# Seven products of quarters for eight in the second products of two feed-forwards, interleaved with the next chunk's first product

## The chip, the cores and the metric

The kernel runs on one core of a Trainium2 chip. The metric is device time in microseconds (us), the median of several executions. Lower is better.

## The reference, cut to what matters

The program is two transformer blocks over 256 tokens with a model width of 2048. Only the two feed-forwards matter here. Everything is float32.

```python
# first block: D_FF = 8192
z = rmsnorm(h, norm2_w) @ mlp_w1                   # 2048 x 8192
h = h + jnp.square(jax.nn.relu(z)) @ mlp_w2        # 8192 x 2048
...
# second block: D_FF_2 = 5632
g, u = jnp.split(x @ w_in, 2, axis=-1)             # 2048 x 11264
y = (jax.nn.silu(g) * u) @ w_out                   # 5632 x 2048
x = layer_norm(ALPHA * x + y, ln_g[l, 2], ln_b[l, 2])
```

## The kernel before

**Float32 in three products.** Every weight and every activation is split into two float32r parts, hi and lo, with hi + lo equal to the value. A product is hi·hi + hi·lo + lo·hi, three matmuls that accumulate in one PSUM bank.

**Weights.** `Stream` (lines 31 to 75) holds the weight tiles in the order in which the products use them, 128 x 1024 elements (two blocks of 128 rows by 512 columns, 512 KB) for nearly all. SyncE loads them into 3 buffers (`RAW`), ScalarE casts a tile to `whi` (line 63), VectorE subtracts to get `wlo` (line 64). There are 4 buffers of each part (`SPLIT`), and splitting runs at most 3 tiles ahead of the products (`LOOK`). So a tile's cast waits until TensorE has finished the tile four places earlier.

**First products** are `TJob`s (lines 221 to 258): weights stationary, out[feature, token]. For a block of 128 rows and 128 features there are two matmuls, one with 512 moving columns (whi times both parts of the tokens, line 257) and one with 256 (wlo times the high part, line 256). A bank is left by `join` (line 351): ScalarE copies one half of it to `ev`, VectorE adds the other half. `relu2` (line 925) then takes relu squared on VectorE and splits the result into `hid`; `gate_f` and `up_f` (lines 1442, 1449) do silu and the product of the second block and split into `fh`. These chains are posts: `side.pump` issues one step of each at a time between the matmuls.

**Second products** are `NJob`s (lines 261 to 317): activations stationary, weights moving, out[token, feature]. One tile takes 12 matmuls of 512 columns (2 row blocks, 2 token tiles of 128, 3 matmuls each, lines 273 to 275). `add_scaled` (line 942), `add_part` (line 938), `first_rows` (line 1466) or `final_rows` (line 1497) add a finished bank to the residual `res` on VectorE.

**Order.** The order of the program is written out by hand in the list `prog`; each engine does its own instructions in that order. The hidden width goes in chunks of 1024 features (8 in the first block, 5 and one of 512 in the second), and chunk c+1's first product stands before chunk c's second product:

```python
    up(0)
    for c in range(NCH):
        if c + 1 < NCH:
            up(c + 1)
        if c == NCH - 1:
            Name(new_xt, "x3t")
        down(c, c == NCH - 1)
```

`last_rows` (line 1470) prepares the last LayerNorm: it clears a tile `gb`, loads ln_g and ln_b rows into it and ln_g for all partitions into `row`, and splits `gb` into `ro`. It is issued before the last but one second product.

## Time and profile before

| | |
|---|---|
| three runs | 2546.81, 2547.54, 2548.10 us (median 2547.54) |
| profiled execution, its span from the first to the last instruction | 2543.4 us |
| what lies around the span, if that execution took the median | 4.1 us |
| TensorE matmul busy | 2520.1 us, 99% of the span |
| VectorE busy | 1611.4 us, 63% |
| ScalarE busy | 1190.8 us, 47% |
| mean granted TensorE clock | 0.997 of full speed |
| bytes moved | 472.93 MB, 186 GB/s |

TensorE's busy time counts overlapping matmuls once and is near 100% wherever matmuls follow each other. How fast they follow is read from their start times. VectorE's mean durations of one instruction are also longer than the step from one to the next where nothing is waited for, since neighbours overlap a little.

### The profile page before, as it was taken

The numbers are of one execution on the slowest core, as the hardware profiler recorded it, in microseconds if no ns is written. First come the engines' busy times: TensorE is split into PE (matmuls) and PEld (weight loads), VectorE is DVE, ScalarE is ACT, GpSimd is POOL, SyncE is SP. The second block draws the span as 40 slices with busy tenths as digits, with TensorE's granted clock in tenths as the row PEclk, the third lists the DMA queues.
The fourth block names the chain that finished last, engine by engine and source line by source line (L and its number), as shares of the span: only waits on it lengthen the run. The fifth ranks groups of instructions, "written<-read, shape, count | busy, mean of one in ns | idle before, by whom it ended". The sixth has DMA issues, their size and how long they took to land.

```text
span 2543.4 us, 34921 instructions
## 1 busy us (share of the span) xinstructions
PE 2520.1 (99%) x13581; PEld 2160.9 (85%) x13581; DVE 1611.4 (63%) x2240; ACT 1190.8 (47%) x1680; POOL 60.6 (2%) x82
## 2 busy tenths in 40 slices
PE   8999999999999999999999999999999999999998
PEld 8897888888888888888888888888788888888886
DVE  5655666556656656768656667767775555565557
ACT  5444444444444444444544565555544444444443
POOL 0000000000000000000000000020200000000000
PEclk9999999999999999999999999999999999999999
DMA  8444555555566565555555555665566666566664
GB/s 278 133 160 147 164 190 189 191 191 191 183 198 197 190 193 190 187 168 181 172 174 166 166 185 188 224 218 165 190 190 190 193 189 195 186 197 189 193 193 156
DMA packets 132326, 472.93 MB, mean 186 GB/s; under 512 B 14992, under 2 KB 16352, under 8 KB 131888
## 3 DMA queue, kind: packets, MB, share of 16 engines
q1 hardware_dynamic: 128624, 460.77, 56.5%
q0 software_dynamic: 3104, 9.32, 1.3%
q8 instruction: 106, 1.74, 0.3%
q10 hardware_dynamic: 432, 0.61, 0.1%
q14 instruction: 60, 0.49, 0.1%
HBM read 468.54 MB, written 2.10 MB: 185 GB/s over the span
## 4 chain that ended last, share of the span: by engine, by line
PE 96%; DVE 2%; DMA 1%; ACT 1%; issue 0%; POOL 0%; SPq 0%; DVEq 0%; ACTq 0%; POOLq 0%
PE acc L257 34%; PE acc L256 17%; PE acc L273 11%; PE acc L274 11%; PE acc L275 11%; PE acc L253 2%; PE acc L247 2%; PE acc L249 2%; PE acc L248 2%; DMA wraw<-in_weights_dram 1%; PE acc L254 1%; DVE wlo L64 1%; PE aux L1160 0%; PE aux L1090 0%; ACT whi L63 0%
## 5 line engine op out<-in xcount | busy, mean ns | idle before, releaser
L64 DVE TENSOR_TENSOR wlo<-wraw,whi 128x1024 fp32r<-128x1024 f32 (+1 forms) x870 | 1055.6, 1219 | 856.0 <-ACT whi L63 854.6
L63 ACT CAST whi<-wraw 128x1024 fp32r<-128x1024 f32 (+1 forms) x870 | 905.8, 1047 | 1060.4 <-PE acc L257 507.7
L257 PE MATMUL acc<-x5t,whi 128*128 128x512 f32 x1320 | 462.8, 394 | 1.0 <-DVE x5t L490 1.0
L256 PE MATMUL acc<-x5t,wlo 128*128 128x256 f32 x1320 | 366.7, 278 | 0.0
L257 PE MATMUL acc<-x3t,whi 128*128 128x512 f32 x960 | 339.4, 395 | 0.0
L257 PE MATMUL acc<-x2t,whi 128*128 128x512 f32 x960 | 335.9, 394 | 0.0
L257 PEld LDWEIGHTS acc<-x5t,whi 128*128 128x128 f32 x1320 | 247.8, 188 | 54.7 <-DVE x5t L490 1.4
L256 PE MATMUL acc<-x3t,wlo 128*128 128x256 f32 x960 | 272.0, 283 | 0.0
L256 PE MATMUL acc<-x2t,wlo 128*128 128x256 f32 x960 | 266.1, 277 | 0.0
L256 PEld LDWEIGHTS acc<-x5t,wlo 128*128 128x128 f32 x1320 | 248.1, 188 | 4.3 <-DVE wlo L64 0.2
L257 PEld LDWEIGHTS acc<-x2t,whi 128*128 128x128 f32 x960 | 180.0, 187 | 39.0
L257 PEld LDWEIGHTS acc<-x3t,whi 128*128 128x128 f32 x960 | 180.1, 188 | 38.6
L273 PE MATMUL acc<-whi,hid 128*128 128x512 f32 x512 | 199.5, 390 | 0.0
L274 PE MATMUL acc<-wlo,hid 128*128 128x512 f32 x512 | 199.2, 389 | 0.0
L275 PE MATMUL acc<-whi,hid 128*128 128x512 f32 x512 | 199.2, 389 | 0.0
L256 PEld LDWEIGHTS acc<-x3t,wlo 128*128 128x128 f32 x960 | 181.0, 189 | 3.2
L256 PEld LDWEIGHTS acc<-x2t,wlo 128*128 128x128 f32 x960 | 180.2, 188 | 2.9
L274 PE MATMUL acc<-wlo,fh 128*128 128x512 f32 x352 | 137.1, 389 | 0.5 <-DVE wlo L64 0.5
L273 PE MATMUL acc<-whi,fh 128*128 128x512 f32 x352 | 137.0, 389 | 0.0
L275 PE MATMUL acc<-whi,fh 128*128 128x512 f32 x352 | 136.9, 389 | 0.0
L275 PEld LDWEIGHTS acc<-whi,hid 128*128 128x128 f32 x512 | 96.1, 188 | 20.0
L274 PEld LDWEIGHTS acc<-wlo,hid 128*128 128x128 f32 x512 | 96.1, 188 | 19.9
(481 smaller groups left out, 3577.5 us busy)
## 6 DMA issues: line engine op xcount, KB each, us to landing
wraw<-in_weights_dram SPq DMA_DIRECT2D x859, 512.0 KB, 3.6
row<-in_ln_g_dram POOLq DMA_DIRECT2D x12, 256.0 KB, 6.5
wraw<-in_weights_dram SPq DMA_DIRECT2D x8, 336.0 KB, 2.9
ht<-in_hT_dram SPq DMA_DIRECT2D x8, 272.0 KB, 5.1
res<-in_x_dram SPq DMA_DIRECT2D x2, 1024.0 KB, 8.6
row<-in_ln_b_dram POOLq DMA_DIRECT2D x8, 256.0 KB, 9.3
out_dram<-res SPq DMA_DIRECT2D x6, 256.0 KB, 2.7
pw<-in_pool_w_dram SPq DMA_DIRECT2D x1, 1024.0 KB, 8.7
```

What stands on the lines that cost most here:

```text
L63: nc.scalar.copy(hi, t)
L64: nc.vector.tensor_tensor(lo, t, hi.bitcast(F32), op=OP.subtract)
L247: mm(b[:m, :n], wh, x[:, 0], start=first, stop=False)
L248: mm(b[:m, :n], wh, x[:, 1], start=False, stop=False)
L249: mm(b[:m, :n], wl, x[:, 0], start=False, stop=last)
L253: mm(bv, wh, x, start=True, stop=False, skip_group_check=True)
L254: mm(bv[:, 1], wl, x[:, 0], start=False, stop=False, skip_group_check=True)
L256: mm(bv[:, 1], wl, x[:, 0], start=False, stop=False, skip_group_check=True)
L257: mm(bv, wh, x, start=False, stop=last, skip_group_check=True)
L273: mm(b, xh, hi[:, j, :n], start=first, stop=False)
L274: mm(b, xh, lo[:, j, :n], start=False, stop=False)
L275: mm(b, xl, hi[:, j, :n], start=False, stop=last)
```

## The change

It replaces the plain second product by one with 7 products of quarters in place of 8. Take 8 row blocks of the hidden features (two halves, A11 A12 over the first 128 tokens, A21 A22 over the others) and 1024 output columns (weight quarters B11 B12 B21 B22, each 4 row blocks by 512 columns). Sums of quarters of A and of B are multiplied, and the seven results are added into the four output quarters, some through a common term `u` that is added at the end. This is done for one of the two column pairs in 7 of the 8 chunks of the first feed-forward and for both pairs in 5 of the 6 chunks of the second, 17 pairs in all.

- A quarter product is two weight tiles ("quarter units") of 6 matmuls each. The four B quarters are loaded into held buffers (`Ring`, five slots, tags g, f0, f1, e3). VectorE adds or subtracts quarters in place (`Stream.sums`, line 85, 128x1024 each, 8 per pair), and each of the 14 units is split into whi and wlo as every tile is (8 tiles per pair before).
- The sums of the hidden features, `four_sums` (lines 516 to 519), are formed on VectorE as features finish, and split by `convert` (lines 1124, 1127) into `spa`, `spb`, `spc` and `l0a`/`l0b`.
- The next chunk's first product is cut into "up units" of one feature block (one tile of 8 row blocks by 128 columns, 16 matmuls). `merge` mixes them with the quarter units; in the first block the last 4 of 16 go with 8 "row units" of the other two column groups, 12 matmuls each.
- Each finished quarter leaves its bank through `put`: 7 VectorE reads per pair where there were 4.
- ALPHA moves into `affine`, which is finished earlier, and `last_rows` now stands right before the last second product.

```diff
+    def pre(self, i):
+        it = self.items[i] if i < len(self.items) else None
+        if isinstance(it, Item) and not it.summed and all(q.t is not None for q in it.quads):
+            self.sums(it.pre)
+            it.summed = True
...
+                    nc.scalar.copy(hi, t)
+                    self.pre(self.s + 1)
+                    nc.vector.tensor_tensor(lo, t, hi.bitcast(F32), op=OP.subtract)
+                    if held:
+                        self.sums(it.post)
...
+        def unit(name, h, bank, first, then):
+            def run():
+                hi, lo = stream.next()
...
+                for j in range(2):
+                    xh, xl = lhs(name, 2 * h + j)
+                    mm(b, xh, hi[:, j], start=first and h == 0 and j == 0, stop=False, skip_group_check=True)
+                    mm(b, xh, lo[:, j], start=False, stop=False, skip_group_check=True)
+                    mm(b, xl, hi[:, j], start=False, stop=h == 1 and j == 1, skip_group_check=True)
+                    if h == 1 and j == 1:
+                        put(then, b)
+                    side.pump()
+            return run
...
+                ("s1", "y", True, "-22", lambda h: Item(b12[h], pre=[(b12[h], b11[h], add)])),
+                ("a11", "x", True, "u", lambda h: Item(b11[h])),
+                ("s2", "u", True, "u+", lambda h: Item(b12[h], pre=[(b12[h], b22[h], add)])),
+                ("s4", "y", False, "-12", lambda h: Item(b22[h])),
+                ("a12", "x", False, "+11", lambda h: Item(b21[h], post=[(b21[h], b12[h], add)])),
+                ("s3", "y", True, "-22", lambda h: Item(b12[h], pre=[(b12[h], b11[h], sub)])),
+                ("a22", "y", False, "+21", lambda h: Item(b21[h]))):
...
+    def merge(head, first, second, tail):
+        n = len(second) - tail
+        done = 0
+        for k, u in enumerate(second):
+            upto = len(first) if k >= n else min(len(first), head + (len(first) - head) * k // max(n - 1, 1))
+            prog.extend(first[done:upto])
+            done = upto
+            prog.append(u)
...
+    def middle(c):
+        Name(set_hid, c + 1, FCH)
+        ups = up_parts(c + 1)
+        down = seven("mlp_w2", FCH * c, 0, mring, lambda name, j: quarter(sums, hid[c], name, j), put_scaled(c))
+        merge(2, ups[:SHARE], down, 0)
+        rows = [u for g in (2, 3) for u in row_units("mlp_w2", FCH * c, g, lambda kb: hid[c][:, kb], add_scaled)]
+        merge(1, ups[SHARE:], rows, 2)
...
+    SEVEN = range(NCH - 1)
+    SHARE = 12
...
+    up()
+    for c in SEVEN:
+        middle(c)
+    Call(add_common_scaled)
+    Name(new_xt, "x3t")
+    down(NCH - 1)
...
+        down = [x for p in range(2) for x in
+                seven("w_ffn_out_2", 8 * c, 1024 * p, ring, lambda name, j: quarter(fh, fh[c], name, j), put_rows(c, p))]
+        merge(2, up_units(c + 1), down, 2)
...
-    ffn_up(0)
-    for c in range(len(chunks)):
-        if c + 1 < len(chunks):
-            ffn_up(c + 1)
-        if c == len(chunks) - 2:
-            Name(last_rows)
-        ffn_down(c)
+    ffn_up()
+    last = len(chunks) - 1
+    Name(lambda: side.finish(tk["affine"]))
+    for c in range(last):
+        ffn_middle(c)
+    Call(add_common)
+    Name(last_rows)
+    n_job("w_ffn_out_2", range(8 * last, 8 * last + 4), grp, lambda kb: fh[last][:, kb - 8 * last], final_rows, tail=2)
```

**Place 1, start of the first feed-forward: VectorE's queue at the end of chunk 0's first product.** `ev` is a feature block just finished, `hid` its split. Before:

```order
L64 TENSOR_TENSOR wlo<-wraw,whi 128x1024 x7
L360 TENSOR_TENSOR ev<-acc,ev 128x256
L928 SCALAR_TENSOR_TENSOR ev<-ev 128x256
L360 TENSOR_TENSOR ev<-acc,ev 128x256
L928 SCALAR_TENSOR_TENSOR ev<-ev 128x256
L373 TENSOR_TENSOR hid<-ev,hid 128x256
```

Now (`l0c` and `l1c` are the earlier feature block put together again from its parts, `sf` the sums of features):

```order
L551 TENSOR_TENSOR hid<-ev,hid 128x256
L1167 TENSOR_TENSOR l1c<-hid 128x256
L516 TENSOR_TENSOR sf<-ev,l1c 128x128
L517 SCALAR_TENSOR_TENSOR sf<-sf,l1c 128x128
L518 SCALAR_TENSOR_TENSOR sf<-ev,sf 128x128
L519 TENSOR_TENSOR sf<-l1c 128x128
L129 TENSOR_TENSOR wlo<-wraw,whi 128x1024
L1127 TENSOR_TENSOR spa<-sf,spa 128x4x128
```

These are the last of four such groups. `spa`, which the first quarter unit s1 reads, stands behind all four; only two up units stand between the end of the first product and s1.

**Place 2, a later chunk of the first feed-forward, around units a12 and s3 of the mixed stretch: VectorE's queue.** Before, at the end of a first product with the whole next group of tiles behind it:

```order
L360 TENSOR_TENSOR ev<-acc,ev 128x256
L928 SCALAR_TENSOR_TENSOR ev<-ev 128x256
L373 TENSOR_TENSOR hid<-ev,hid 128x256 x2
L64 TENSOR_TENSOR wlo<-wraw,whi 128x1024 x7
L360 TENSOR_TENSOR ev<-acc,ev 128x256
```

Now (`quads` and `quad...` are the held B quarters, L85 their sums, L1215 a put):

```order
L129 TENSOR_TENSOR wlo<-quads,whi 128x1024
L85 TENSOR_TENSOR quads<-quads,quade_4127 128x1024
L551 TENSOR_TENSOR hid<-ev,hid 128x256
L129 TENSOR_TENSOR wlo<-quads,whi 128x1024
L85 TENSOR_TENSOR quads<-quads,quade_4127 128x1024
L1215 SCALAR_TENSOR_TENSOR res<-aux_4406,nr,res 128x512
L85 TENSOR_TENSOR quade_4127<-quade_4127,quadf_3476 128x1024
L129 TENSOR_TENSOR wlo<-wraw,whi 128x1024
```

Sums, a put and posts now stand between the wlo of one tile and that of the next.

**Place 3, the end of the second feed-forward: VectorE's queue.** Before, the preparation of the last LayerNorm stood among the posts of the last first product, a whole second product earlier:

```order
L360 TENSOR_TENSOR ev<-acc,ev 128x256
L1452 TENSOR_TENSOR ev<-ev,sg 128x256
L1477 MEMSET gb 64x2048
L1483 MEMSET l0a 128x64
L1484 MEMSET l0a 128x1
```

Now the last s3 and a22 (`aux_22431` is their bank; a22's matmuls add into it behind the put of L1841):

```order
L129 TENSOR_TENSOR wlo<-wraw,whi 128x1024
L538 TENSOR_TENSOR ev<-acc,ev 128x256
L1803 TENSOR_TENSOR ev<-ev,l1c 128x256
L1841 SCALAR_TENSOR_TENSOR res<-aux_22431,res 128x512
L129 TENSOR_TENSOR wlo<-wraw,whi 128x1024
L551 TENSOR_TENSOR fh<-ev,fh 128x256
L129 TENSOR_TENSOR wlo<-wraw,whi 128x1024
L1839 TENSOR_TENSOR res<-aux_22431,res 128x512
L1849 TENSOR_TENSOR res<-res,l1a 128x512 x3
L1849 TENSOR_TENSOR res<-res,l1b 128x512 x3
L1865 MEMSET gb 64x2048
```

and behind the small memsets:

```order
L129 TENSOR_TENSOR wlo<-wraw,whi 128x1024 x2
L1888 TENSOR_TENSOR res<-acc,res 128x512
L1891 BN_STATS st<-res 128x6
L1893 TENSOR_TENSOR res<-res,row 128x512
L1888 TENSOR_TENSOR res<-acc,res 128x512
```

The product with `row` (L1893) waits for a load that GpSimd issues behind the five loads into `gb`, which wait for the memset. In all 13407 matmuls become 13203.

## Rows read from the trace of the kernel before

**Rows 1.** Page, part 1: span; busy time, share and instructions of each engine.

```profile
span 2543.4 us, 34921 instructions
...
PE 2520.1 (99%) x13581; PEld 2160.9 (85%) x13581; DVE 1611.4 (63%) x2240; ACT 1190.8 (47%) x1680; POOL 60.6 (2%) x82
```

**Rows 2.** Page, part 4: chain of waits that ended last, share by engine.

```profile
PE 96%; DVE 2%; DMA 1%; ACT 1%; issue 0%; POOL 0%; SPq 0%; DVEq 0%; ACTq 0%; POOLq 0%
```

**Rows 3.** Busy time by stretch, the two feed-forwards: length, PE, PEld, DVE, ACT, POOL, clock.

```profile
352.00:1042.00 690.00, 690.00 (x3520) 587.34 (x3519) 425.61 (x522) 306.42 (x391) 0.00 (x0) 1.00 0.59 190
1830.00:2490.00 660.00, 660.00 (x3536) 567.66 (x3535) 387.73 (x470) 303.19 (x408) 4.60 (x9) 1.00 0.61 192
```

**Rows 4.** Timeline of TensorE, second product: start, us; 21 matmuls from first to last.

```profile
1000.24 0.39 PE L273 MATMUL acc<-whi,hid 128*128 128x512 f32 x1
...
1005.00 0.39 PE L273 MATMUL acc<-whi,hid 128*128 128x512 f32 x1
```

**Rows 5.** Timeline of TensorE, first product: 16 pairs apart, then the next job's start.

```profile
374.91 0.40 PE L257 MATMUL acc<-x2t,whi 128*128 128x512 f32 x1
...
380.45 0.40 PE L257 MATMUL acc<-x2t,whi 128*128 128x512 f32 x1
...
382.07 0.39 PE L253 MATMUL acc<-x2t,whi 128*128 128x512 f32 x1
```

**Rows 6.** VectorE by line and shape: count, busy us, mean ns, idle before.

```profile
L64 DVE TENSOR_TENSOR wlo<-wraw,whi 128x1024 fp32r<-128x1024 f32 x859 | 1047.0, 1224 | 849.6 <-ACT whi L63 848.2
...
L944 DVE SCALAR_TENSOR_TENSOR res<-acc,rq,res 128x512 f32<-128x512 f32 x56 | 39.3, 743 | 0.0
...
L1379 DVE TENSOR_TENSOR res<-res,row 128x512 f32<-128x512 f32 x16 | 10.9, 684 | 0.0
...
L1104 DVE TENSOR_TENSOR pb<-pb,l1b 128x128 f32<-128x128 f32 x1 | 0.3, 292 | 0.0
```

**Rows 7.** Timeline of VectorE, instructions behind each other without a wait.

```profile
2471.96 3.50 DVE L64 TENSOR_TENSOR wlo<-wraw,whi 128x1024 fp32r<-128x1024 f32 x3 [0.52 <-ACT whi L63]
2475.38 1.28 DVE L940 TENSOR_TENSOR res<-acc,res 128x512 f32<-128x512 f32 x2
```

**Rows 8.** Timeline of VectorE, end of the first feed-forward's first t_job.

```profile
381.73 0.42 DVE L360 TENSOR_TENSOR ev<-acc,ev 128x256 f32<-128x256 f32 x1
...
382.52 0.42 DVE L360 TENSOR_TENSOR ev<-acc,ev 128x256 f32<-128x256 f32 x1
...
383.32 0.42 DVE L373 TENSOR_TENSOR hid<-ev,hid 128x256 fp32r<-128x256 f32 x1
383.65 0.42 DVE L360 TENSOR_TENSOR ev<-acc,ev 128x256 f32<-128x256 f32 x1
...
385.10 1.23 DVE L64 TENSOR_TENSOR wlo<-wraw,whi 128x1024 fp32r<-128x1024 f32 x1 [0.57 <-ACT whi L63]
```

**Rows 9.** Timeline of ScalarE, the same place.

```profile
383.43 0.41 ACT L371 CAST hid<-ev 128x256 fp32r<-128x256 f32 x1
...
384.01 1.05 ACT L63 CAST whi<-wraw 128x1024 fp32r<-128x1024 f32 x1
```

**Rows 10.** Busy time by stretch around a LayerNorm; the last but two number is the clock.

```profile
1790.00:1794.00 4.00, 1.34 (x8) 0.87 (x8) 2.83 (x7) 1.78 (x5) 2.69 (x3) 1.00 0.00 0
1794.00:1798.00 4.00, 3.68 (x15) 3.18 (x14) 2.83 (x7) 3.36 (x7) 4.00 (x4) 0.57 0.00 0
```

**Rows 11.** Timeline of VectorE: the memset and the split for the last LayerNorm.

```profile
2466.00 1.76 DVE L1477 MEMSET gb<- 64x2048 f32 x1 [0.37 <-issue]
...
2489.83 2.28 DVE L1493 TENSOR_TENSOR ro<-gb,ro 32x2048 fp32r<-32x2048 f32 x1
```

**Rows 12.** Timeline of GpSimd: its loads for the last LayerNorm.

```profile
2468.05 1.00 POOL L183 DMA_DIRECT2D gb<-in_ln_g_dram  x2 [661.79 <-DVE l1a L1483]
...
2470.47 2.18 POOL L183 DMA_DIRECT2D row<-in_ln_g_dram  x4
```

**Rows 13.** Page, part 6: issues, KB each, us to landing.

```profile
row<-in_ln_g_dram POOLq DMA_DIRECT2D x12, 256.0 KB, 6.5
```

More of the change, by code (lines that the diff above doesn't have):

```diff
@@ L74, in next @@
             self.fill()
+        assert self.i <= self.s
         return self.parts.pop(self.i - 1)
@@ new lines, in seven, with run @@
+    def seven(W, k0, c0, ring, lhs, put):
+        b12, b11, b22, b21 = ring.quads(W, k0, c0)
+        add, sub = OP.add, OP.subtract
+        at = {}
+        def unit(name, h, bank, first, then):
+            def run():
+                hi, lo = stream.next()
+                if first and h == 0:
+                    at[bank] = acc() if bank == "u" else aux(0 if bank == "y" else 1)
+                b = at[bank]
+                for j in range(2):
[5 more added lines that the diff above has]
+                        put(then, b)
+                    side.pump()
+            return run
+        out = []
+        for name, bank, first, then, item in (
+                ("s1", "y", True, "-22", lambda h: Item(b12[h], pre=[(b12[h], b11[h], add)])),
[5 more added lines that the diff above has]
+                ("a22", "y", False, "+21", lambda h: Item(b21[h]))):
+            for h in range(2):
+                out.append(Unit(item(h), unit(name, h, bank, first, then)))
+        return out
@@ new lines, in put_gate, with f, put_up @@
+    def put_gate(i):
+        def f(b):
+            d = fh["sg", i] = tmp(i % 2, "c", [128, SEQ])
+            yield from join(d, b)
+            yield
+            S.activation(d, d, AF.Silu)
+        return f
+    def put_up(c, i, pair, last):
+        def f(b):
+            z = yield from join(None, b)
+            V.tensor_tensor(z, z, fh["sg", i], op=OP.mult)
+            yield from split_steps(fh[c][:, i, 0], fh[c][:, i, 1], z)
+            if not pair:
+                return
+            if i < 4:
+                fh["z"] = z
+                return
+            yield
+            four_sums(fh["sf"], i - 4, fh["z"], z)
+            if last:
+                yield from convert(fh)
+        return f
@@ new lines, in up_units, with put_rows, f @@
+    def up_units(c):
+        g0, n = chunks[c]
+        order = [i + 4 * k for i in range(4) for k in range(n)]
+        out = []
+        for i in order:
+            c0 = 512 * g0 + 128 * i
+            out += feature_units("w_ffn_in_2", c0, xt("x5t"), put_gate(i))
+            out += feature_units("w_ffn_in_2", FF + c0, xt("x5t"), put_up(c, i, n == 2, i == order[-1]))
+        return out
+    ring = Ring(new_slots(lambda: side.finish(tk["affine"])))
+    def put_rows(c, p):
+        def f(what, b):
+            u = fh["u"][p]
+            if what == "u" and c == 0:
+                V.tensor_copy(u, b)
+            elif what[0] == "u":
+                V.tensor_tensor(u, b, u, op=OP.add)
+            else:
+                r = res[:, int(what[1]) - 1, 1024 * p + 512 * (int(what[2]) - 1):][:, :512]
+                if what[0] == "+":
+                    V.tensor_tensor(r, b, r, op=OP.add)
+                else:
+                    V.scalar_tensor_tensor(r, b, -1.0, r, op0=OP.mult, op1=OP.add)
+        return f
```

316 lines of the change are left out of this document (260 added, 56 removed).

## The prediction

> **What bounds the kernel now.** I read the page's busy shares first: TensorE 99% of the 2543.4 us span, VectorE 63% [rows 1]. The chain of waits says the same: 96% of it is TensorE [rows 2]. Then I look whether that holds in the stages that change: in both feed-forwards TensorE is busy without a gap (690 of 690 and 660 of 660 us), VectorE 426 of 690 and 388 of 660 us [rows 3]. So today a matmul taken away is time gained, and VectorE has some 38 to 41% to spare. The question is whether that room is enough, and in the right places.
>
> **The price of a matmul.** In a second product 21 steps take 1005.00 - 1000.24 = 4.76 us, 0.2267 each [rows 4]. A pair of matmuls of the first product takes (380.45 - 374.91)/16 = 0.346 [rows 5]. So an up unit (8 pairs) is 2.77 us, a quarter unit (6 matmuls) 1.36, a row unit (12) 2.72. **Gain:** 7 products for 8 saves 12 matmuls per pair, 17 pairs, 204 matmuls, which is also what the two counts of matmuls differ by: 204 x 0.2267 = 46.2 us. DMA bytes stay the same.
>
> **The price of VectorE's work.** A wlo takes 1224 ns [rows 6], but three behind each other take 3.50 us: the step is (3.50 - 1.22)/2 = 1.14, and two bank reads of 512 step by 1.28 - 0.68 = 0.60 [rows 7]; neighbours overlap by 0.08. A put with a scale is 0.743 [rows 6], a step of 0.66. A sum of weight quarters is not in the trace. Its nearest row is the add of 512, 684 ns [rows 6]: twice that, 1.37, is the upper end, the lower is that it costs nothing where VectorE would idle; by the wlo of the same size I take 1.14. A join with its follower steps by 0.79 and a split by 0.33 [rows 8]. A 128-wide operation is 0.29 [rows 6]; four_sums is four, two of which need the one before: 2 x 0.21 + 2 x 0.32 = 1.06.
> The Trainium skill, "VectorE: DVE Perf Modes", section Terms, says that the next operation can't issue until the pipe is empty. By that rule each step would be the whole duration. Rows 7 disagree: three durations of 1.22 fit in 3.50.
>
> **Part 1, the mixed stretch of the first feed-forward** (7 chunks). TensorE: 12 x 2.77 + 14 x 1.36 = 52.3 us. VectorE, instructions of that stretch: 26 wlo 29.6, 6 of the 8 sums 6.8 (two stand before it), 5 scaled puts and 2 plain ones 4.5, 6 feature chains 6 x 1.13 = 6.8, three four_sums 3.2: 50.9 us. That alone is 97%. But VectorE also idles inside. A feature's cast on ScalarE waits for VectorE's chain, and the next tile's whi stands behind that cast: 0.31 (the cast less its overlap) + 1.05 + 0.04 until the wlo may start, some 1.4 [rows 8, 9], less what VectorE has to do in between. Going down the queue of place 2's stretch, that is 1.4 for two of the six chains, 0.9 and 0.8 twice for three, 0.3 for one: 5.5 us. 50.9 + 5.5 = 56.4 against 52.3. The look-ahead of three tiles holds 1.36 to 2.77 us each, so it gives way first at the clusters. I walked the queue with these steps from a stretch that begins with VectorE caught up: the fourth wlo finishes 0.7 us before its use, then TensorE waits 1.2 us at the up unit before s4, 2.5 at the one behind a12 (three sums and a put stand before its wlo, place 2), 0.6 and 0.2 at the next two, and 1.0 at a22, whose bank s3's put must leave first. **5.5 us per chunk**, 3.5 in the seventh, which forms no sums for the eighth: 36.5 us. Ends: 0, if the look-ahead swallows it, and 7.5 per chunk if nothing overlaps better than in my walk. I take the walk's value, since every step of it has a row. The second stretch of a chunk (4 up units, 8 row units, 32.9 us) needs 22 us of VectorE and is covered.
>
> **Part 2, the two starts.** In both feed-forwards' chunk 0 the sums are formed from a whole t_job at once (place 1). The chain starts on VectorE at 381.73 and the next job's first matmul stands at 382.07 [rows 5, 8]. Until spa is whole, VectorE has 4 x 0.79 + 4 x 0.33 + 4 adds of hi and lo (0.45, each needs the one before) + 4 x 1.06 + a little for dependences 0.3 + two wlo 2.28 + spa itself 0.6: 13.6, so 395.3 us. TensorE has two up units (5.54) and the first two matmuls of s1 (0.45) until 388.1. **Wait 7.2 us, twice: 14.4.** After some 5 us in which TensorE did 1.34 us of work, the clock stood at 0.57 over the next 4 us [rows 10], partly the lower of its two levels (1.2 of 2.4 GHz): 4 x 0.43 = 1.7 us lost. I add it twice: 3.4. Ends: 4 (if posts overlap better) and 10 each.
>
> **Part 3, the chunk ends of the second feed-forward** (5). The last three quarter units, s3's second and a22's two, stand without an up unit between them. a22 adds into the bank that s3's put must read, and in VectorE's queue a wlo, a join and a product stand before that put (place 3). From the start of s3's last unit: copy and whi on ScalarE until 1.6, wlo 1.14, chain 0.79, put 0.74: 4.3. TensorE would be ready at 1.36. **3.0 us, five times: 15.0.** Ends 1.0 (put alone) and 4.5.
> Elsewhere the second feed-forward mixes 32 up units with 28 quarter units, 126.7 us of TensorE; VectorE: 60 wlo and 16 sums 86.6, puts 8.8, chains 11.7, four_sums and converts 6.7: 113.8, 90%; my walk through its first half meets no wait. Its last chunk has only 16 up units: about 2.86 us of TensorE per quarter unit against 2.92 of VectorE plus ScalarE waits: 5 us (0 to 9).
>
> **Part 4, the tail.** last_rows now stands at the start of the last second product (8 tiles, 21.8 us). From its start: put until 1.2, common sums 3.7, memset 1.76 and small ones until 7.1 [rows 11], two wlo, an add and a bn_stats until 10.8. GpSimd's five loads of `gb` wait for the memset (at 6.7), 0.5 each, then `row` is issued at 9.4 and lands 6.5 later [rows 12, 13]: 15.9. Only then come the product with `row`, the second evacuation and the sixth tile's wlo, until 19.6, while TensorE would start that tile at 13.6: 5.7 us. The split of `ro` (2.28 [rows 11]) and two more evacuations delay the last two tiles by 0.9 and 3.6. **10.2 us.** Ends 4 and 13.
> ALPHA in affine, the earlier finish of affine (50 steps against 96 pumps) and the adds of u at the first block's end lie beside TensorE work: nothing, 1 us if uncovered.
>
> **Sum.** -46.2 + 36.5 + 14.4 + 3.4 + 15.0 + 5 + 10.2 = +38.3 on the profiled execution's 2543.4 us span. With the 4.1 us around a span that stands for the median of 2547.5: **2585.8 us, slower by 1.5%.**
>
> **Rivals.**
> 1. *TensorE still sets the end in the mixed stretches* (the look-ahead covers them and the last chunk): -41.5, 2544.3 us, no clear change. For: VectorE idles 38% now [rows 3], 50.9 is less than 52.3. Against: the ScalarE waits inside.
> 2. *Faster: the change works as counted.* The mixed stretches are covered, the puts at chunk ends come early (1.0 each), the clock stays up and the tail costs 4: -46.2 + 14.4 + 5 + 4 = -22.8, about 2525 us. It decides from the point where VectorE's queue is less than 52.3 us per stretch, waits included. Against it is the order: spa stands behind all four groups in any case.
> 3. *The clock falls after each wait.* About 11 waits of 2.5 to 3 us would each bring 1.7 us of lower clock: +19, 2605 us. For: rows 10. Against: there TensorE was nearly idle for longer. No row of before shows a wait of this size, so it keeps a chance.
> 4. *No overlap on VectorE*: 69 instructions per mixed stretch x 0.08 = 5.5 us more in each of 7, 38.6 in all: 2624 us. Against: rows 7. This is the rule of the Trainium skill weighed above.
>
> That fewer matmuls are left out than said is excluded by the counts.
>
> **Chances.** Forecast 0.55 (its own range 2562 to 2605), rival 1 0.19, rival 2 0.16, rival 3 0.07, rival 4 0.03. The range 2540 to 2605 leaves out rival 2, and rivals 3 and 4 in large part. About 0.2% (5.1 us) is what a measurement of this kernel can tell from no change. Faster by more than that: rival 2 and a small part of rival 1, 0.19. Within: the middle of rival 1, 0.11. Slower: the rest, 0.70.
>
> **What would show it.** In the profile after: TensorE idle before `spa` in chunk 0 of both feed-forwards, released by VectorE, 7 us each; idle before `wlo` in the mixed stretches, 5 us per chunk, VectorE over 95% busy there; idle before a22 at each chunk end of the second feed-forward, 3 us, released by the put; idle of VectorE on a `row` load in the last 25 us. If TensorE's idle in the mixed stretches is under 1 us per chunk, Part 1 is wrong; if the total of such idle is under 46 us, the sign is.

## The result, and the profile after

The changed kernel takes 2657.1 us (median of 4 runs, 2652.0 to 2661.1) against 2547.2, a ratio of 1.043 (95% interval 1.0417 to 1.0447): slower by 110 us. The direction was the one forecast; the size was not: 38 us were forecast, and 2657 lies outside the range. The profiled execution has a span of 2650.2 us, 106.8 more than before.

The page of the changed kernel, its busy times and its chain by engine, answers to [rows 1, 2]:

```profile
span 2650.2 us, 35211 instructions
...
PE 2546.7 (96%) x13377; PEld 2146.5 (81%) x13377; DVE 1983.7 (75%) x2800; ACT 1305.2 (49%) x1842; POOL 59.7 (2%) x82
...
PE 81%; DVE 11%; issue 3%; ACT 3%; DMA 2%; POOL 0%; SPq 0%; DVEq 0%; ACTq 0%; POOLq 0%
```

TensorE has 204 matmuls less and is busy for 27 us more. That is the first sign of something that a sum of waits doesn't hold. Its share of the chain fell from 96 to 81%; 11% now are VectorE's.

Busy time by stretch (length, PE, PEld, DVE, ACT, POOL, clock, DMA share, GB/s) of the first feed-forward, four chunks of the second, and the end, against [rows 3]:

```profile
352.00:1089.00 737.00, 701.53 (x3437) 579.67 (x3436) 590.98 (x796) 357.90 (x468) 2.20 (x4) 0.99 0.53 179
1885.00:2545.00 660.00, 630.79 (x3265) 531.46 (x3263) 552.81 (x702) 344.22 (x466) 0.00 (x0) 0.98 0.54 187
2545.00:2640.00 95.00, 76.09 (x324) 60.10 (x325) 76.79 (x102) 34.44 (x40) 9.70 (x15) 0.92 0.29 98
```

TensorE is no longer busy throughout in either stage, VectorE went from 62 to 80% and from 59 to 84%, and the granted clock is no longer 1.00. What TensorE waited for is in the waits of the changed kernel (engine, tile, line, releaser: us in total, times, longest):

```profile
PE aux L482 <- DVE res L1841: 20.2, 6, 3.5
PE acc L432 <- DVE wlo L129: 16.8, 8, 2.4
PE aux L482 <- ACT spa L1124: 12.0, 2, 6.4
PE acc L434 <- DVE wlo L129: 10.8, 13, 1.6
PE aux L482 <- DVE res L1839: 7.0, 5, 1.7
...
PE acc L342 <- DVE wlo L129: 5.4, 2, 3.3
PE aux L1931 <- DVE l0c L1914: 2.6, 1, 2.6
```

From the top: a22 behind s3's put at the chunk ends of the second feed-forward, an up unit behind its wlo in the mixed stretches, s1 behind `spa` at the two starts, the second of a feature's two up units behind its wlo, s1 behind the put of the a22 before it, and the end.

Then the starts of TensorE's matmuls. In the second product the steps were 0.2267 us [rows 4]; in the changed kernel's last plain second product (21 steps between these two):

```profile
1059.77 0.39 PE L341 MATMUL acc<-whi,hid 128*128 128x512 f32 x1
...
1064.66 0.40 PE L341 MATMUL acc<-whi,hid 128*128 128x512 f32 x1
```

That is 4.89 us, 0.2329 each. The code of this product is unchanged. So are the stages far from the change: a product with `mg` between the two feed-forwards shows the same.

Added up over the trace, from the starts of neighbouring matmuls (steps over 0.6 us count as waits, less an ordinary step; steps of 0.29 to 0.6 are listed apart), the 106.8 us are:

| part | forecast | measured |
|---|---|---|
| matmuls left out, 204 | -46.2 | -46.2 |
| waits, first feed-forward | 36.5 + 7.2 = 43.7 | 39.8 |
| waits, second feed-forward and end | 7.2 + 15 + 5 + 10.2 = 37.4 | 54.8 - 6.0 before = 48.8 |
| single longer steps, most at the lower clock (0.29 to 0.6 us; 0.2 in place of 0.12 behind 256 columns) | 3.4 | 12.0 + 18.4 = 30.4 |
| ordinary steps longer, all three stages | 0 | 14.4 + 8.2 + 12.5 = 35.1 |
| sum | 38.3 | 107.9 |

The waits came as forecast within 8 us in sum; 4 us less in the first feed-forward and 11 more in the second partly cancel, which is luck. Two terms were missing: the length of every step, and most of the lower clock.

### The profile page after: what moved, and what is told of

It reads as the page before. It is cut to its first block, busy times and chain, and to the rows that moved or that the text cites. A ratio compares the mean times of both kernels' runs of the same rounds, so it can differ in the third digit from the quotient of the medians.

```text
span 2650.2 us, 35211 instructions
## 1 busy us (share of the span) xinstructions
PE 2546.7 (96%) x13377; PEld 2146.5 (81%) x13377; DVE 1983.7 (75%) x2800; ACT 1305.2 (49%) x1842; POOL 59.7 (2%) x82
## 4 chain that ended last, share of the span: by engine, by line
PE 81%; DVE 11%; issue 3%; ACT 3%; DMA 2%; POOL 0%; SPq 0%; DVEq 0%; ACTq 0%; POOLq 0%
PE acc L325 15%; PE acc L435 13%; PE acc L324 8%; PE acc L434 7%; DVE wlo L129 6%; PE acc L341 4%; PE acc L343 4%; PE acc L342 4%; PE aux L482 3%; PE aux L484 3%; PE aux L483 2%; ACT whi L127 2%; PE acc L1239 2%; PE acc L1237 2%; PE acc L1238 2%
## 5 line engine op out<-in xcount | busy, mean ns | idle before, releaser
L129 DVE TENSOR_TENSOR wlo<-wraw,whi 128x1024 fp32r<-128x1024 f32 (+2 forms) x734 | 888.7, 1216 | 493.1 <-ACT whi L127 491.7
L127 ACT CAST whi<-wraw 128x1024 fp32r<-128x1024 f32 (+2 forms) x734 | 760.5, 1043 | 576.6 <-PE acc L325 226.6
L435 PE MATMUL acc<-x5t,whi 128*128 128x512 f32 x1080 | 387.6, 397 | 0.0
L325 PEld LDWEIGHTS acc<-x3t,whi 128*128 128x128 f32 x960 | 180.5, 188 | 39.4
L524 ACT COPY ev<-acc 128x256 f32<-128x256 f32 x256 | 94.2, 371 | 164.6 <-PE acc L435 145.3
L129 DVE TENSOR_TENSOR wlo<-quads,whi 128x1024 fp32r<-128x1024 f32 x96 | 117.0, 1221 | 37.5 <-ACT whi L127 36.8
L129 DVE TENSOR_TENSOR wlo<-quadf,whi 128x1024 fp32r<-128x1024 f32 x92 | 112.1, 1220 | 29.7 <-ACT whi L127 29.3
L127 ACT CAST whi<-quads 128x1024 fp32r<-128x1024 f32 x96 | 100.0, 1046 | 51.6 <-DVE quads L85 32.5
L127 ACT CAST whi<-quadf 128x1024 fp32r<-128x1024 f32 x92 | 95.7, 1045 | 40.2 <-DVE quadf L85 28.3
L315 PE MATMUL acc<-x1t,whi 128*128 128x272 f32 (+1 forms) x336 | 100.0, 298 | 5.8 <-ACT whi L127 5.8
L317 PE MATMUL acc<-x1t,wlo 128*128 128x272 f32 (+1 forms) x336 | 97.3, 289 | 0.4 <-DVE wlo L129 0.4
L316 PE MATMUL acc<-x1t,whi 128*128 128x272 f32 (+1 forms) x336 | 97.1, 289 | 0.0
```

What stands on the lines that cost most here:

```text
L127: nc.scalar.copy(hi, t)
L129: nc.vector.tensor_tensor(lo, t, hi.bitcast(F32), op=OP.subtract)
L315: mm(b[:m, :n], wh, x[:, 0], start=first, stop=False)
L316: mm(b[:m, :n], wh, x[:, 1], start=False, stop=False)
L317: mm(b[:m, :n], wl, x[:, 0], start=False, stop=last)
L325: mm(bv, wh, x, start=False, stop=last, skip_group_check=True)
```

## Experiments

The stage times below run from the first matmul with `x2t` to the last with `hid` (before: 706.7 us, after: 753.6), and from the first with `x5t` to the last of all (741.4 and 793.6).

### Is it the chip or the program, and which part?

`e1_before` and `e1_after` are the two kernels unchanged. `e1_first_only` gives the second feed-forward its plain t_jobs and second products back, `e1_second_only` the first:

```diff
+    SEVEN = ()
...
+    for c in range(NCH - 1):
+        up(c + 1)
+        n_job("mlp_w2", range(FCH * c, FCH * c + FCH), grp,
+              lambda kb, c=c: hid[c][:, kb - FCH * c], add_scaled)
```

> The kernel before, unchanged, beside itself. In the profile of the changed kernel every matmul with 512 moving columns steps by 0.233 us where it was 0.2267, in stages that the change does not touch too. Theory A (the step belongs to the changed program): this run shows 0.2267 in the product with mixp again, 2547 us. Theory B (the step belongs to the chip or the execution): on this chip it shows 0.233 too, about 2585 us, in the runs of before beside it as well.

Measured: 2546.4 us, ratio 0.9995 (0.9986 to 1.0004). The product with `mg` steps by (1654.33 - 1649.80)/20 in its timeline:

```profile
1649.80 0.39 PE L274 MATMUL acc<-wlo,mg 128*128 128x512 f32 x1
...
1654.33 0.39 PE L273 MATMUL acc<-whi,mg 128*128 128x512 f32 x1
```

0.2265 us. The same product in the changed kernel, 20 steps again:

```profile
1699.82 0.40 PE L343 MATMUL acc<-whi,mg 128*128 128x512 f32 x1
...
1704.48 0.40 PE L342 MATMUL acc<-wlo,mg 128*128 128x512 f32 x1
```

0.2330. So the step belongs to the changed program (theory A).

> The changed kernel once more, on the same chip as the kernel before. Theory A: step 0.233 in the product with mixp and 2657 us, a ratio of 1.043. Theory B: the step is that of the kernel before on this chip, and the ratio falls towards 1.027, what waits (92 us), lower clock (some 20 us) and the 46.2 us gained leave.

Measured: 2657.3 us, ratio 1.0432 (1.0415 to 1.0449). Theory A again.

> The seven products in the first feed-forward alone. From the changed kernel's profile: 84 matmuls fewer -19.0 us, waits 39.7, lower clock about 8, together 2576 us if the step of a matmul stays at 0.2267; 38 us more, 2614, if the first feed-forward's part is what makes every matmul step by 0.233. My forecast's own terms for this part: -19.0 + 36.5 + 7.2 + 1.7 = 2574 us.

> The seven products in the second feed-forward alone. From the changed kernel's profile: 120 matmuls fewer -27.2 us, waits 53, lower clock about 12, together 2585 us with a step of 0.2267; 2623 if this part brings the step of 0.233. My forecast's own terms for this part: -27.2 + 7.2 + 1.7 + 15 + 5 + 10.2 = 2559 us.

Measured: 2618.2 us (1.0262 to 1.0293) and 2622.2 (1.0279 to 1.0309). Each part alone costs 71 and 75 us, together 145, while the whole change costs 110. Some 36 us are there with either part and only once: both have the step of 0.233 in every stage.

### The place in memory

What both parts have in common is small: `square_scale` makes two new tiles, `nr`, of 32 bytes per partition each, for the negative scale. They are allocated ahead of the large pool, and so everything in it lies 64 bytes later (from the built programs, bytes from the start of a partition):

```
tile            before          after
whi (first)     28800           28800
x2t, x5t        128896          128960
hid, fh         188800, 172416  188864, 172480
```

`e2_before_shift` moves the kernel before by as much, with no other instruction:

```diff
-                r = small("rq", [128, 1], bufs=2)
+                r = small("rq", [128, 16], bufs=2)[:, 0:1]
```

`e2_aligned` puts the changed kernel's `nr` beside `rq` in one tile:

```diff
-                r = small("rq", [128, 1], bufs=2)
+                both = small("rq", [128, 2], bufs=2)
+                r = both[:, 0:1]
...
-                n = small("nr", [128, 1], bufs=2)
```

> The kernel before with each of two small tiles 32 bytes longer, so that every tile of the large pool (features, hidden features, residual) starts 64 bytes later, as in the changed kernel; no instruction differs. Theory P (where the operands lie sets the matmul's step): 0.233 us in the product with mixp and in the second products, and some 3700 steps x 6.6 ns plus 3700 first-product pairs x 4 ns, 39 us in all: 2586 us. Rival Q (the step comes from the changed program's instructions): 0.2267 and 2547 us.

Measured: 2582.5 us, ratio 1.0142 (1.0127 to 1.0157): 36 us for 64 bytes, and nothing else. The second product of the first feed-forward (21 steps):

```profile
1000.20 0.40 PE L273 MATMUL acc<-whi,hid 128*128 128x512 f32 x1
...
1005.10 0.39 PE L273 MATMUL acc<-whi,hid 128*128 128x512 f32 x1
```

4.90 us, 0.2333 each, at the same lines that stepped by 0.2267 [rows 4]. Theory P holds.

> The changed kernel with its two new small tiles laid into two that are there already, so that the large pool starts where it does in the kernel before; the same instructions. Theory P: step 0.2267 again, 2657 - 38 = 2619 us. Rival Q: 0.233 and 2657 us. What is left over the kernel before is then the waits and the clock: 92 + 20 - 46 = 66, 2613 us.

Measured: 2641.7 us (1.0360 to 1.0394). The product with `mg`, 20 steps:

```profile
1699.66 0.39 PE L341 MATMUL acc<-whi,mg 128*128 128x512 f32 x1
...
1704.19 0.39 PE L343 MATMUL acc<-whi,mg 128*128 128x512 f32 x1
```

The step is 0.2265 again, but only 16 of the 38 us came back. By the starts, ordinary steps took 17 us less; the up units had not changed (0.352 a pair in either place), and steps at the lower clock took 4 us more in the first feed-forward. The waits stayed: 39.4 us in the first feed-forward and 56.0 in the second.

### The order of the first product

`e3_units_plain` has no seven products at all, but from the second chunk on the up units in place of the t_jobs, with the large pool where it was before:

```diff
+        prog.extend(up_parts(c + 1))
         n_job("mlp_w2", range(FCH * c, FCH * c + FCH), grp,
```

> No seven products: plain second products of 8 tiles per group in both feed-forwards, memory as in the kernel before, but the first products of the later chunks in up units (one feature block, 16 matmuls on one bank) in place of four features at a time. Up units step by 0.352 us per pair in the changed kernel, with the old place in memory too, where the t_jobs step by 0.347. Theory U (this order of the first product costs 5 ns per pair by itself): 2048 pairs x 5.3 ns = 11 us, 2558 us. Rival (the longer step comes from what stands beside the up units in the changed kernel): 2547 us.

Measured: 2559.0 us, ratio 1.0051 (1.0036 to 1.0066), 13 us. Five pairs of an up unit, without a wait anywhere near:

```profile
404.61 0.28 PE L434 MATMUL acc<-x2t,wlo 128*128 128x256 f32 x1
...
406.38 0.28 PE L434 MATMUL acc<-x2t,wlo 128*128 128x256 f32 x1
```

1.77/5 = 0.354, where a t_job has 0.346 [rows 5]. Theory U holds: in this order a pair takes longer. An up unit sends 16 matmuls to one bank, over eight blocks of x2t, and the feature's second unit 16 more to the same bank; a t_job sends four to each of four banks, over two blocks. The weight blocks also lie otherwise in their tile (128 columns apart, against 512). Which of the three makes the difference, the bank, the change of block or the place of the weights, isn't told apart here.

### VectorE's queue

`e3_no_sums` leaves out the 136 weight sums. `e3_sums_pool` gives them to GpSimd. Both stand on `e2_aligned`.

```diff
-            self.nc.vector.tensor_tensor(to.t, to.t, frm.t, op=op)
+            self.nc.gpsimd.tensor_tensor(to.t, to.t, frm.t, op=op)
```

> The changed kernel in its old place in memory, without the 136 weight sums of 128x1024 (left out altogether: the weight quarters of s1, s2, s3 and a22 are then plain quarters). Theory V (VectorE's queue sets the mixed stretches): 9.1 us per pair go from it, so the 5 us of waits per chunk of the first feed-forward fall under 1.5, the spa waits of the second vanish, and with them some 10 us of lower clock: 2642 - 28 - 6 - 10 = 2598 us or less. Rival (the waits are chains of one tile or one feature, whatever the queue holds): 2630 us or more.

Measured: 2587.6 us (1.0151 to 1.0181), 54 less than with them. In the first feed-forward the waits fell from 39.4 to 13.3 us and the steps of 0.29 to 0.6 from 16.3 to 4.7. In the second the waits fell by 7 alone, from 56.0 to 48.7. So theory V holds for the first; what the second waits for is something besides. A sum is also a link in the chain ahead of its tile's cast, and this run takes away both. That the load of the queue counts by itself is shown by the row units moved between the quarter units below: there all sums stay, and the waits of the first feed-forward fall to 23.1 us (`e2_first_mixed`) and to 11.5 (`e4_all_woven`).

> The same kernel with the weight sums on GpSimd, the result complete. A product of 128x512 takes 1.29 us there, so a sum of 1024 about 2.5, 20 us per pair beside 52 us. Theory V: nearly what leaving them out gives, 2600 us. Rival L (a sum of 2.5 us before a cast is a longer chain than the look-ahead covers, or GpSimd holds VectorE up): 2640 us or more.

Measured: 2778.8 us (1.0900 to 1.0933): 137 us worse than on VectorE. Groups of that trace (count, busy us, mean ns, idle before):

```profile
L129 DVE TENSOR_TENSOR wlo<-quadf,whi 128x1024 fp32r<-128x1024 f32 x92 | 138.3, 1507 | 52.7 <-ACT whi L127 50.5 <-PE aux L484 1.9
...
L85 POOL TENSOR_TENSOR quadf<-quadf,quads 128x1024 f32<-128x1024 f32 x30 | 87.1, 2911 | 284.0 <-DVE wlo L129 277.8 <-issue 6.1
```

A sum takes 2.9 us in place of 1.2 and waits for the wlo that still reads its quarter, so the next cast comes later than the look-ahead covers. And a wlo that runs beside a sum is longer:

```profile
602.27 3.42 DVE L129 TENSOR_TENSOR wlo<-quads,whi 128x1024 fp32r<-128x1024 f32 x1
...
601.29 3.31 POOL L85 TENSOR_TENSOR quadf<-quadf,quadf 128x1024 f32<-128x1024 f32 x1 [3.09 <-DVE wlo L129]
```

The mean of 1507 ns hides two kinds. Of the 961 wlo of this shape, 108 overlap a sum on GpSimd, and 83 of these take 1.5 to 3.4 us; the 853 others take 1.22 us on average, as all do with the sums on VectorE. The Trainium skill, "SBUF — State Buffer", section Who interferes with whom, says that a VectorE instruction with two inputs in SBUF contends with a GpSimd instruction that reads SBUF. The trace agrees, by these 83.

`e3_all_pool` had the sums on GpSimd as well, with the repairs of the next section. It was expected at 2550 us, or at 2590 and more if GpSimd's sums hold the chain up; it took 2722.4 (1.0677 to 1.0713), with 70.8 us of waits in the first feed-forward and 83.3 in the second. The repairs don't make up for the slower sums.

### The order of the units

`e2_first_mixed` puts the 8 row units of a chunk between its quarter units, and makes chunk 0's last four features one after the other. It stands on `e2_aligned`, as do all runs of this section:

```diff
-        merge(2, ups[:SHARE], down, 0)
-        merge(1, ups[SHARE:], rows, 2)
+        merge(2, ups, weave(down, rows), 2)
```

> On top of the last: in the first feed-forward the 8 row units stand between the quarter units (all 16 up units over both), and in chunk 0 the last four features are made one after the other. Theory (VectorE's queue is full in the mixed stretch and nearly idle in the second one): VectorE's 73 us and TensorE's 85 us lie in one stretch, the waits of 5 us per chunk go, and the 5.9 us at the start fall to under 1.5: 2615 - 36 - 6 - 5 of lower clock = 2570 us. Rival (each wait is the latency of one chain, whatever the load): over 2600 us.

Measured: 2619.1 us (1.0269 to 1.0299). The first feed-forward fell from 750.0 to 728.5, not to 703: at the start the waits fell from 6.9 to 3.8 us, and in the later chunks one of 1.6 stayed behind a12. The row units were spread evenly and VectorE's work isn't; `e4_first_woven` below tries whether that is the reason.

`e2_second_mixed` changes the second feed-forward: an up unit before each unit of a22, chunk 0's last features one after the other, seven products for one pair alone in the last mixed chunk (12 matmuls more), and an earlier last_rows:

```diff
+            upto = min(len(ups), 4 + round((len(ups) - 4) * k / 26))
...
+    Call(last_rows)
+    prog.insert(-2, prog.pop())
```

> On top of the placement alone: in the second feed-forward an up unit stands before each of the two units of a22, chunk 0's last features are made one after the other, the last but one chunk takes seven products for one pair alone and row units for the other (12 matmuls more, 2.7 us), and the last LayerNorm's rows are loaded two row units earlier and first. Theory: 3.7 us at five chunk ends, 6.8 at the start, 10 in the last but one chunk, 10 at the end and some 10 of lower clock go, 2.7 come: 2615 - 52 = 2563 us. Rival (VectorE is full in the whole stage, so what goes here comes back at the next chunk's spa): no more than 15 us less, 2600 us.

Measured: 2617.9 us (1.0265 to 1.0296), 24 less, between the theory's 52 and the rival's 15. The 3.7 us at the chunk ends became 0.8, but new waits of 0.5 to 1.8 stand at up units and at `spa`: from 56.0 to 41.9 us in all. The rival's mechanism is there in part: VectorE hands some of the waits on.

`e4_all_no_sums` has both and no weight sums (they are left out); `e4_all_woven` has both with the sums, and the row units after the first weights where VectorE has most to do; `e4_first_woven` has the first feed-forward's part of that, and plain products in the second. Against the placing in `e2_first_mixed`:

```diff
-            if i % 2 and i < 12:
+            if i in (1, 5, 8, 9, 10, 11):
```

> All repairs together (memory as before, row units between quarter units, features of chunk 0 one after the other, up units before a22, one pair in the last but one chunk, earlier last rows), and the weight sums left out. Theory V (VectorE's queue is what is left): 2588 of the changed kernel without sums, less some 23 for each feed-forward's repairs, not more than what is left of waits there: about 2550 us. Rival (the quarter units' own chains set the end): 2575 us or more.

Measured: 2540.5 us, ratio 0.9976 (0.9966 to 0.9985). The second feed-forward's waits are 15.4 us here, against 48.7 without the repairs and 41 with the repairs and the sums: neither cure does it alone. With some 146 us of VectorE's work taken away (the 128 sums of its 16 pairs x 1.14), and a result that is therefore another, the seven products would be faster, by 0.24%.

> All repairs together with the weight sums on VectorE and the result complete; the row units of the first feed-forward and of the last but one chunk now stand where VectorE's queue is fullest (after the second unit of s1 and of s2, both of a12 and both of s3). If the two feed-forwards' repairs add up: 2642 - 23 - 24 = 2595 us, and the placing of the row units takes away most of the 1.85 us that is left behind a12 in each chunk, some 12 us: 2583 us. If VectorE's queue only hands the wait on: 2595 us or more.

> The same in the first feed-forward alone, with plain second products in the second one. The first feed-forward took 706.7 us before and 728.5 with the row units evenly spread; with 12 us less, 716, and the second one as before: 2546 + 10 = 2556 us. It would beat the kernel before only if the waits left (23 us) and the lower clock (10 us) went altogether: 2535 us.

Measured: 2582.3 us (1.0125 to 1.0155) and 2556.9 (1.0025 to 1.0055). Both as expected: the repairs add up, and the placing of the row units gave 15 us in the first feed-forward (713.7).

`e5_first_late` starts the seven products at chunk 1; `e5_one_pair` adds seven products for one pair per chunk of the second feed-forward:

```diff
-    SEVEN = range(NCH - 1)
+    SEVEN = range(1, NCH - 1)
```

> As the last run (seven products in the first feed-forward alone, repaired), but from the second chunk on: chunk 0 has a plain second product, so no sums are formed from a whole t_job. 12 matmuls come back (2.7 us); the start's 3.8 us of waits and 1.7 us of lower clock go: 2557 - 5.5 + 2.7 = 2554 us. Rival: the start and the late weight load of the second chunk (7 us with its lower clock) only move on by one chunk: 2560 us.

> The same, and in the second feed-forward seven products for one of the two column pairs of each chunk, row units for the other, the row units where VectorE's queue is fullest. VectorE has some 96 us of work beside 129 of TensorE per chunk there. Theory V: no waits of over 1 us at the chunk ends; 5 x 2.72 = 13.6 us of matmuls fewer, 6.3 us for the up units' longer step, some 2 at the start and the end: 2554 - 5 = 2549 us, no change from the kernel before. Rival (the chunk ends cost whatever VectorE's load is): 2565 us or more.

Measured: 2551.1 us, ratio 1.0016 (1.0007 to 1.0025), and 2563.1 (1.0050 to 1.0075). The first is the nearest that a complete version came; what is left there is 7.8 us of waits, 6.2 of them in one place, where the chain of `e4_first_woven` shows a late weight tile:

```profile
461.99 10.17 DMA wraw<-in_weights_dram
```

Such a load takes 3.5 us as a rule; it moved with the start by one chunk, as the rival said. Why it is late was not tried. In the second kernel the chunk ends have no waits left but one of 0.5 us, as theory V said; but its second feed-forward is 756.5 us, 10.7 more than the plain one of `e5_first_late` (745.8). By the starts, 60 matmuls fewer give 13.6 us. Against that stand some 9 us more of waits (one more late load, 10.65 us in its chain, and an end with 10 us of waits), 7 of lower clock, most of it behind these, 6 for the up units' longer pair and 2 in the quarter units' steps. The waits at the start of that feed-forward are nearly the same in both kernels. No complete version beats the kernel before.

### Waits and the clock

`e4_bursts` puts waits into the kernel before, by forming 15 of the wlo several times over:

```diff
+BURST = {112 + 16 * i: (6, 7, 8, 9, 10)[i % 5] for i in range(15)}
...
-                nc.vector.tensor_tensor(lo, t, hi.bitcast(F32), op=OP.subtract)
+                for _ in range(1 + BURST.get(self.s, 0)):
+                    nc.vector.tensor_tensor(lo, t, hi.bitcast(F32), op=OP.subtract)
```

> The kernel before with 15 bursts on VectorE in the first feed-forward: at every sixteenth weight tile its wlo is formed 6, 7, 8, 9 or 10 times more (the same values). TensorE has three tiles of 2.72 us ahead, so by 1.14 us each the waits would be about 0.8, 2, 3.1, 4.3 and 5.4 us, three of each: 47 us. Theory C (a wait of about 3 us or more brings TensorE's lower clock for some matmuls, 1.5 us lost each time, one of 2.5 us sometimes, a shorter one never): 9 to 11 times 1.5 us more, 2546 + 47 + 15 = 2608 us, and rows at the lower clock stand behind the long waits alone. Rival (the lower clock in the changed kernel comes from its mix of instructions): no row at the lower clock here, 2593 us.

Measured: 2639.7 us (1.0347 to 1.0377). The waits were longer than expected (67.5 us in all, each about 1.2 more), and so was what followed them. The stretches behind a wait of 3.0, of 4.3 and of 6.9 us; the clock is the last but two number:

```profile
430.10:434.10 4.00, 3.86 (x22) 3.45 (x23) 2.35 (x3) 0.00 (x0) 0.00 (x0) 1.00 0.68 207
...
478.40:482.40 4.00, 3.88 (x9) 3.11 (x10) 3.65 (x5) 0.10 (x1) 0.00 (x0) 0.50 0.49 156
...
832.60:836.60 4.00, 3.83 (x12) 3.35 (x13) 2.38 (x3) 0.00 (x0) 0.00 (x0) 0.50 0.61 199
```

All nine waits of 4.26 us or more are followed by matmuls at the lower of the two levels, 10 to 18 of them, 1.6 to 2.9 us lost each time (20.8 us in all). None of the seven of 1.7 to 3.1 us is. So a wait alone brings the clock down (theory C), without the change's mix; in this first feed-forward all waits of 4.26 us and more do, and none of up to 3.1 us. The Trainium skill, "TensorE: Matmul & The Clock Gate", section HAM oscillation, describes this: each long enough wait on data returns the engine to the slow state, and the next stretch of work pays for it. The rows of `e4_bursts` agree.

The length alone doesn't decide it, though. In `e2_aligned` the first four chunk ends of the second feed-forward bring the same wait, 3.7 us; three are followed by the lower clock and one isn't:

```profile
2348.80:2352.80 4.00, 3.80 (x12) 3.08 (x13) 3.93 (x9) 2.41 (x3) 0.00 (x0) 0.71 0.69 228
...
2485.20:2489.20 4.00, 3.77 (x18) 3.25 (x19) 3.93 (x9) 2.50 (x3) 0.00 (x0) 1.00 0.72 223
```

In that kernel a wait of 2.0 us behind the first a12 is followed by 12 matmuls at the lower clock. In `e3_no_sums` six waits of 2.9 us stand at chunk ends, with no other wait of over 0.4 us in the 20 us before; five are followed by the lower clock.

## Why the prediction was right and wrong

**Right: the order of the queues.** Part 2 had `spa` whole at 395.3 us. VectorE in the changed kernel, from the first join of chunk 0's last features to that place:

```profile
381.90 0.42 DVE L538 TENSOR_TENSOR ev<-acc,ev 128x256 f32<-128x256 f32 x1
...
393.48 0.28 DVE L519 TENSOR_TENSOR sf<-l1c 128x128 f32<-128x128 f32 x1
393.68 1.22 DVE L129 TENSOR_TENSOR wlo<-wraw,whi 128x1024 fp32r<-128x1024 f32 x1
394.81 0.68 DVE L1127 TENSOR_TENSOR spa<-sf,spa 128x512 fp32r<-128x512 f32 x1
```

It ends at 395.49. TensorE started s1 at 393.6, when the high part was there, and stopped again for the low one: 5.7 + 1.1 us, against 7.2. The second start took 6.6 + 1.1.

Part 1 had 2.5 us behind a12 for three sums and a put ahead of a wlo. In the third chunk, VectorE and then TensorE:

```profile
614.17 1.23 DVE L85 TENSOR_TENSOR quade<-quade,quadf 128x1024 f32<-128x1024 f32 x1
...
616.90 1.22 DVE L85 TENSOR_TENSOR quade<-quade,quadf 128x1024 f32<-128x1024 f32 x1
618.04 0.74 DVE L1215 SCALAR_TENSOR_TENSOR res<-aux,nr,res 128x512 f32<-128x512 f32 x1
618.70 1.21 DVE L85 TENSOR_TENSOR quadf<-quadf,quads 128x1024 f32<-128x1024 f32 x1
619.83 1.22 DVE L129 TENSOR_TENSOR wlo<-wraw,whi 128x1024 fp32r<-128x1024 f32 x1
```

```profile
618.39 0.40 PE L431 MATMUL acc<-x2t,whi 128*128 128x512 f32 x1
621.10 0.38 PE L432 MATMUL acc<-x2t,wlo 128*128 128x256 f32 x1 [2.32 <-DVE wlo L129]
```

A step of 2.71, 2.5 over an ordinary one, in five of seven chunks (2.0 and 1.8 in the first and the last). Before s4 the waits were 1.3 to 1.5 (forecast 1.2), at a22 0.9 in three chunks and none in the others (forecast 1.0). In all 29.8 us of the 36.5, besides 3.1 at a late load that no step had. One of the signs that the prediction named did not come: VectorE over 95% busy in these stretches. From the first matmul of s1 to the last of a22 it is 88%:

```profile
586.10:639.80 53.70, 49.12 (x246) 40.20 (x245) 47.13 (x60) 26.41 (x34) 0.00 (x0) 1.00 0.51 178
```

The prediction's own figures say as much: 50.9 us of work in 52.3 + 5.5 of waits are 88%; its sign goes by 50.9 of 52.3, without the waits. A sum steps by 1.14 (616.90 to 618.04), the value taken for an operation that the trace of before didn't have.

Part 3 had 3.0 us at each chunk end. TensorE and VectorE at the first of them:

```profile
2084.31 0.40 PE L484 MATMUL aux<-whi,l0b 128*128 128x512 f32 x1
2088.24 0.77 PE L482 MATMUL aux<-whi,fh 128*128 128x512 f32 x1 [3.53 <-DVE res L1841]
```

```profile
2083.20 2.36 DVE L129 TENSOR_TENSOR wlo<-quads,whi 128x1024 fp32r<-128x1024 f32 x2 [1.42 <-ACT whi L127]
2085.47 1.22 DVE L129 TENSOR_TENSOR wlo<-wraw,whi 128x1024 fp32r<-128x1024 f32 x1
2086.61 0.42 DVE L538 TENSOR_TENSOR ev<-acc,ev 128x256 f32<-128x256 f32 x1
2087.06 0.42 DVE L1803 TENSOR_TENSOR ev<-ev,l1c 128x256 f32<-128x256 f32 x1
2087.40 0.68 DVE L1841 SCALAR_TENSOR_TENSOR res<-aux,res 128x512 f32<-128x512 f32 x1
```

3.7 us at each of the first four chunk ends; the last mixed chunk has two such waits, 3.5 and 2.9. VectorE idles for 1.42 us on ScalarE's cast, and then three wlo stand ahead of the join, the product and the put, where Part 3 had one. Also, s1 of the next chunk waits 1.5 us for the put of a22 (four times 1.5), which the walk through that stage's first half did not meet. The last mixed chunk took 6 us besides its ends, for 5.

Part 4's row load shows as VectorE's idle time, and the split of `ro` ahead of a wlo as TensorE's:

```profile
2618.57 0.69 DVE L1893 TENSOR_TENSOR res<-res,row 128x512 f32<-128x512 f32 x1 [5.08 <-DMA row<-in_ln_g_dram]
...
2622.49 2.28 DVE L1881 TENSOR_TENSOR ro<-gb,ro 32x2048 fp32r<-32x2048 f32 x1
```

12.5 us of waits from there to the end, where the kernel before had 4.1: 8.4 more, of the 10.2.

**Wrong: "The price of a matmul".** The step 0.2267 and the pair 0.346 were read in the kernel before and used for every matmul that stays, as if the change could only take matmuls away. Both prices moved: the second product's step to 0.233, by 64 bytes that two small tiles put ahead of the pool (e2_before_shift: 36 us on the kernel before), and the first product's pair to 0.352, by the cut into up units (e3_units_plain: 13 us). The two don't add up where they meet, in the up units (0.352 a pair in either place); together the ordinary steps took 35.1 us more. "An up unit (8 pairs) is 2.77 us" was the second of these in plain sight: a new form of an old operation was priced as the old one. This is the step of the prediction that failed: it put the change of these two prices at nothing, without a reason, and they make 35.1 us. No rival had either.

**Wrong in size: the lower clock, 30.4 us for 3.4.** The forecast had it at the two starts alone, 3.4 us, and rival 3 had it after every wait, 19 more, at 0.07. Measured are runs of 6 to 16 slow matmuls after the starts, three of the five waits of 2.5 us behind a12, every wait of 3.5 us and more in the second feed-forward, and at the end: 22 us, and some 8 in single longer steps. So rival 3 had the size of this term nearly right. Three stretches of the changed kernel, each right behind a wait of 2.5 us:

```profile
528.20:532.20 4.00, 3.92 (x15) 3.45 (x16) 3.65 (x6) 1.91 (x4) 0.00 (x0) 0.58 0.39 133
...
621.00:625.00 4.00, 3.90 (x21) 3.31 (x21) 3.64 (x6) 1.92 (x4) 0.00 (x0) 1.00 0.43 133
...
806.60:810.60 4.00, 3.93 (x16) 3.42 (x17) 3.65 (x6) 1.91 (x4) 0.00 (x0) 0.68 0.43 133
```

The same wait at the same place of a chunk brings the lower clock in one chunk and not in the next, while the lone waits of 3.0 us in `e4_bursts` never did. A wait of 1.3 to 1.5 us ends some 14 us before each of the five, so waits shortly before don't tell them apart. Nor does the program: in `e1_after`, the same kernel once more, three of the five are followed by the lower clock again, but not the same three. What decides it stays open.

Rivals 1 and 2 fell with Part 1. Rival 4 (no overlap on VectorE) fell with the sums' step of 1.14.

## What to carry to other kernels

Before anything is summed, compare where the tiles of both versions lie: two new tiles of a few bytes ahead of a large pool moved every operand behind them, and lengthened matmuls all over the program. When a trace of the changed kernel is there, look first at the step of an unchanged product, and only then at waits. And a trade of matmuls for VectorE's work is to be counted as what stands ahead of which wlo: here 2.7 us of TensorE per pair were bought with 6 wlo, 8 sums and 3 puts, some 18 us, on an engine whose room lay in other places than its new work.

## What the runs showed of the hardware that was not expected

- With the stationary activations (second products) or the moving ones (first products) 64 bytes later in every partition, and the weights where they were, a matmul of 512 columns steps by 0.2333 us in place of 0.2267, a first-product pair by 0.351 in place of 0.347. In the first place the addresses are multiples of 128 bytes, in the second odd multiples of 64. The whole pool moved, other engines' operands with it. Other offsets weren't tried.
- The first product's pair takes 0.352 to 0.354 us with 16 matmuls on one bank and eight blocks in turn, 0.346 with four matmuls on a bank and two blocks, at the full clock and without a wait (`e3_units_plain`; the weight blocks lie otherwise too).
- A wlo of 1.22 us takes 1.5 to 3.4 when it overlaps a sum on GpSimd (83 of 108 in `e3_sums_pool`); the means of 1.45 to 1.52 mix these with the others.
- In the first feed-forward of `e4_bursts` seven waits of 1.7 to 3.1 us left the clock up and nine of 4.26 to 6.9 us brought it down. In other kernels single waits of 2.0 to 3.7 us did either, the same wait at the same place included (`e2_aligned`, `e3_no_sums`, the changed kernel and `e1_after`).
